# Attention scores of a hybrid decoder layer: two full-array matmuls in place of row-tiled passes

## The chip, the core and the metric

The kernel runs on one core of a Trainium2 chip. Five engines work side by side: TensorE (PE, the matrix engine, whose weight loads are listed apart as PEld), VectorE (DVE), ScalarE (ACT), GpSimd (POOL) and SyncE (SP), which here issues the DMAs. The metric is device time in microseconds of the whole program; lower is better. The times given are medians of separate runs, and a profile is one execution, so the two differ slightly.

## What is computed

One decoder layer on 1024 tokens of width 1024 in float32. One input projection feeds two token mixers, differential attention and a Mamba-2 state-space scan (SSD); their outputs are gated, merged and projected back. The change touches the scores of the attention:

```python
q = rms_norm(q, q_norm_w)            # 8 heads x 2 maps, 64 features each
k = rms_norm(k, k_norm_w)
scores = jnp.einsum('bqhmd,bkhmd->bhmqk', qb, k) * ATTN_HEAD_DIM ** -0.5
scores = jnp.where(causal, scores, -jnp.inf)
p = jax.nn.softmax(scores, axis=-1)
a = p[:, :, 0] - lam * p[:, :, 1]
o = jnp.einsum('bhqk,bkhe->bqhe', a, v)
```

Each head has two maps (m = 0 and 1), each with its own 64 query and 64 key features, so a score has a contraction of only 64, while TensorE's array has 128 rows.

## The kernel before

**Exact parts.** Matmuls are to be as good as float32. A float32 value is split into a high part that the engine's one-pass format (`F32R`) holds exactly and a low part that is the difference, and a product is made of three matmuls: high by high, high by low, low by high (`mm3`, `steps3`). ScalarE makes the high part by a copy, VectorE the low part by a subtraction.

**Order.** All instructions are issued in an order that a planner, class `Plan`, works out while the program is built. Its clock `pl.t` is TensorE's: every `mm` (line 162) and `tp` (a transpose, line 171) adds its cost. `bulk` (line 1197) supplies the large projections; chains of small steps (attention, SSD, splitting of weights) are generators that yield the time at which their next step falls due, and a step that is due goes ahead of the bulk work. Buffers are rationed on the same clock by class `Slots`: `bigs` counts the 19 large SBUF tiles of 4 KB per partition (`NBIG`, line 33), `mids` the medium ones, `trs`, `scs` and `mms` the PSUM tiles for transposes, scores and projections, two of each. The engines themselves then run their queues in this order and wait only for their operands.

**Stages.** The projections of the eight attention heads come first, `att_proj(h)` (line 470): for each of eight token tiles, 24 matmuls of 512 columns into a PSUM tile `pma`, which holds q, k, v and the gate of the head. While head h is projected, the attention of the heads before runs between its matmuls. Then come the four SSD groups: `ssd_proj_z` (PSUM tile `pmz`, four large tiles `zs`), `ssd_proj_xbc` (PSUM tiles `pc`, six large tiles `cv`), and beside the next group's projections `ssd_core`, eight chunks, each with a large decay tile `ab` and a product in PSUM tile `pD`. Last come the gates (`pg`), the merged projections (`pf`) and the output projection (`po`); line 1156 makes the last tile of `po` in two halves.

**Attention of a head.** `att_evac` (line 497) copies a projected tile out and normalises q and k. `qk_stack` (line 518) runs for each half of the tokens (512): it transposes q and k to feature-major in a PSUM tile `pq`, whose partitions 0 to 63 belong to map 0 and 64 to 127 to map 1, and fills the operands of the scores. `att_proj` reserves seven large tiles for a head: `v`, `zg` (the gate), `qs` and `kh` for both maps, and `kl`. They are given back when the last block of the head is done.

- `qs[m]` stacks the high and the low part of q of map m over the 128 partitions (high on the map's own 64, low on the other 64).
- `kh[m]` has the high part of k of map m twice, once on each half of the partitions.
- `kl` has the low part of k, map 0 on partitions 0 to 63, map 1 on 64 to 127.

`att_core` (line 553) then spawns `att_block` for each of the four query blocks of 128 tokens in the half. A block (line 562) takes keys up to its own end, n = 128 to 1024 columns, in column blocks of up to 512 (lines 584 to 590): per map one matmul of `qs` and `kh` over all 128 rows, which gives high by high and low by high at once, and then per map one matmul of 64 rows, high part of q by `kl`. The two 64-row matmuls use different halves of the array's rows. After that VectorE masks the scores and finds the row maximum (line 572), ScalarE takes the exponential, the two maps are combined, transposed (`pa`), multiplied with `v` (`av`), normalised, gated and transposed (`pya`).

Of the kernel before, what the change touches and what calls it, by code (L numbers as in the profile page):

```python
# [8 lines left out]
F32 = mybir.dt.float32  # L9
F32R = mybir.dt.float32r  # L10
BF16 = mybir.dt.bfloat16
AF = mybir.ActivationFunctionType
ALU = mybir.AluOpType
AX = mybir.AxisListType

P = 128
S = 1024
# [12 lines left out]
C_ZS = 7168  # L30
C_DT = 9216
C_GATE = 9248
NBIG, NW, NRAW, NMID, NSM = 19, 9, 4, 12, 8
PACE = 13.0
WPOOL = 3
XAHEAD = 3
HOP = 0.12
# [1 line left out]


class Slots:
    """Reuse times of a ring of buffers on the planned clock."""

    def __init__(self, n):
        self.free = [0.0] * n
# [11 lines left out]


class Plan:
    """One order for all engines: steps of dependent chains as their inputs fall due on a planned  # L60
    clock (the tensor engine's), bulk matrix work between them."""

    def __init__(self):
        self.t = 0.0
# [42 lines left out]
def tile_hybrid_layer(ctx: ExitStack, tc: tile.TileContext, x, norm_w, w_in, q_norm_w, k_norm_w,  # L107
                      diff_lambda, subln_w, conv_w, conv_b, dt_bias, a_log, d_skip, ssd_norm_w,
                      w_proj_attn, w_proj_ssd, w_out, out):
    nc = tc.nc  # L110
# [3 lines left out]
    const = ctx.enter_context(tc.tile_pool(name="const", bufs=1))  # L114
# [16 lines left out]

    pl = Plan()
    bigs, mids, sms = Slots(NBIG), Slots(NMID), Slots(NSM)
    trs, scs, mms = Slots(2), Slots(2), Slots(2)
    ws, raws = Slots(NW), Slots(NRAW)

    def bigt(shape, dt=F32, name="b"):
        return big.tile(shape, dt, tag="b4", name=name)
# [19 lines left out]
    def hpt(name):  # L158
        return hpool.tile([P, KB, S], F32R, tag="h", name=name)

# [1 line left out]
    def mm(o, lhsT, rhs, start, stop, after=0.0):  # L162
        nc.tensor.matmul(o, lhsT=lhsT, rhs=rhs, start=start, stop=stop)  # L163
        n, m = rhs.free_size(), lhsT.free_size()
        if rhs.dtype == F32:
            c = max(4 * n / 2400, 0.215)
        else:
            c = max(n / 2400 + 0.003, 0.057 if m <= 64 else 0.107)
        pl.t = max(pl.t, after) + c
# [13 lines left out]
    def in_ps(*aps):  # L183
        return any(a.space == bass.MemoryType.PSUM for a in aps)

    def act(o, i, f, after, **kw):
        nc.scalar.activation(o, i, f, **kw)  # L187
        c = 0.83e-3 * i.free_size() + (0.052 if in_ps(i) else 0.093) + 0.093 * (("accum_out" in kw) + any(not isinstance(kw.get(i, 0.0), float) for i in ("scale", "bias")))
        return pl.op("A", c, after)

    def tt(o, a, b, op, after, eng="V"):
        (nc.vector if eng == "V" else nc.gpsimd).tensor_tensor(out=o, in0=a, in1=b, op=op)  # L192
        n = o.free_size()
        return pl.op(eng, 0.07 + 1.042e-3 * n if eng == "V" else 0.095 + (1.77e-3 if op == ALU.mult else 2.22e-3) * n, after)

    def stt(o, a, s, b, op0, op1, after):
        nc.vector.scalar_tensor_tensor(out=o, in0=a, scalar=s, in1=b, op0=op0, op1=op1)  # L197
        return pl.op("V", 0.07 + 1.042e-3 * o.free_size() + (0.0 if isinstance(s, float) else 0.06), after)
# [21 lines left out]
        nc.gpsimd.tensor_tensor(out=dst, in0=dst, in1=mhalf[:, 0:cols], op=ALU.pow)  # L220
        return pl.op("G", 0.55 + 0.18 * cols, after)

# [1 line left out]
    mhalf = const.tile([P, 4], F32, name="mhalf")  # L224
    nc.gpsimd.memset(mhalf, -0.5)
    ident = const.tile([P, P], F32, name="ident")
# [12 lines left out]
    snc = lambda b: cols2[:, b:b + 1]  # L239
    sub_c, wqk_c, nlam_c = cols2[:, 16:17], cols2[:, 19:20], cols2[:, 20:21]  # L240
    hH, hL = hpt("hH"), hpt("hL")
    ready = {}

    def consts():
# [38 lines left out]
        trs.give(k, t1)  # L283
        ready["consts"] = stt(cols2[:, 19:20], cols2[:, 17:18], 8.0, cols2[:, 18:19], ALU.mult, ALU.mult, t1)

# [1 line left out]
    def att_w(h):  # L287
        return [(w_in[kb * P:(kb + 1) * P, 0:4096].rearrange("p (f c) -> p f c", f=4)[:, :, h * P:(h + 1) * P], 4, P)
                for kb in range(KB)]
# [84 lines left out]
        mm(o, a[1], b[0], False, last)  # L374
        yield

# [1 line left out]
    xts = {}  # L378
    h_at = {}

# [82 lines left out]
            if last and kb % 4 == 3:  # L463
                w_done(ids[kb // 4])

# [1 line left out]
    hd = {}  # L467
    lefts = {}

    def att_proj(h):  # L470
        ids = w_next(KB)
        ks = []
        for _ in range(7):
            ks.append((yield from pl.get(bigs)))
        v = bigt([P, NT, P], name=f"v{h}")
        zg = bigt([P, NT, P], name=f"zg{h}")
        qs = [bigt([P, S], F32R, name=f"qs{h}{m}") for m in range(2)]
        kh = [bigt([P, S], F32R, name=f"kh{h}{m}") for m in range(2)]
        kl = bigt([P, S], F32R, name=f"kl{h}")
        hd[h] = (v, zg, qs, kh, kl, ks)  # L480
        lefts[h] = [NT, {}]
        qk = []
        for t in range(NT):
            k = yield from pl.get(mms)
            pm = mmt(f"pma{h}{t}")
            yield from proj_tok(pm, t, ids, t == NT - 1)
            if t % 2 == 0:
                km = yield from pl.get(mids)
                qk.append([midt([P, 2, 256], name=f"qk{h}{t}"), km, 0])
            pl.spawn(att_evac(h, t, pm, k, qk[-1][0][:, t % 2, :], qk[-1]), pe_done())  # L490
            if t % 4 == 3:
                pl.spawn(qk_stack(h, t // 4, qk), pl.t + 3.0)
                qk = []
            if h == 0 and t == 0:
                pl.spawn(consts())
# [20 lines left out]
        cell.append(t2)  # L516

    def qk_stack(h, half, qk):
        v, zg, qs, kh, kl, _ = hd[h]
        lo, hi = slice(0, 64), slice(64, P)  # L520
        cs = slice(half * 512, half * 512 + 512)
        while len(qk[0]) < 5 or len(qk[1]) < 5 or "consts" not in ready:
            yield pl.t + 0.2
        yield max(qk[0][3:] + qk[1][3:] + [ready["consts"]])
        done = []
        for isk in range(2):
            k = yield from pl.get(trs)
            pt = trt(f"pq{h}{half}{isk}")
            for i in range(4):
                tp(pt[:, i * P:(i + 1) * P], qk[i // 2][0][:, i % 2, isk * P:(isk + 1) * P])  # L530
            if isk:
                for c in qk:
                    mids.give(c[1], pl.t + 0.1)
            at = pe_done()
            yield at
            t1 = at
            for m, (own, other) in enumerate(((lo, hi), (hi, lo))):
                if isk:
                    act(kh[m][own, cs], pt[own], AF.Copy, at)
                    t1 = act(kh[m][other, cs], pt[own], AF.Copy, at)  # L540
                else:
                    t1 = act(qs[m][own, cs], pt[own], AF.Copy, at, scale=wqk_c[own])
            yield t1
            for m, (own, other) in enumerate(((lo, hi), (hi, lo))):
                if isk:
                    t1 = tt(kl[own, cs], pt[own], kh[m][own, cs], ALU.subtract, t1 - HOP)
                else:
                    t1 = stt(qs[m][other, cs], pt[own], wqk_c[own], qs[m][own, cs], ALU.mult, ALU.subtract, t1 - HOP)
            done.append(t1)
            trs.give(k, t1)  # L550
        pl.spawn(att_core(h, half), max(done))

    def att_core(h, half):
        for qb in range(half * 4, half * 4 + 4):
            while max(bigs.avail(2), scs.avail(2)) > pl.t:
                a = max(bigs.avail(2), scs.avail(2))
                yield a if a < INF else pl.t + 0.2
            pk = [bigs.take(), bigs.take()]
            pl.spawn(att_block(h, qb, pk))
            yield pl.t + 0.6  # L560

    def att_block(h, qb, pk):
        v, zg, qs, kh, kl, ks = hd[h]
        n = (qb + 1) * P
        qsl = slice(qb * P, n)
        pr, sums, ex = [], [], []

        def soft(m, sc, k, at):
# [14 lines left out]
        sc = [sct(f"sc{h}{qb}{m}") for m in range(2)]  # L583
        for j in range(0, n, 512):
            e = min(n, j + 512)
            for m in range(2):
                mm(sc[m][:, j:e], qs[m][:, qsl], kh[m][:, j:e], True, False)
            for m in range(2):
                own = slice(m * 64, m * 64 + 64)
                mm(sc[m][:, j:e], qs[m][own, qsl], kl[own, j:e], False, True)  # L590
        for m in range(2):
            pl.spawn(soft(m, sc[m], k[m], pe_done()), pe_done() + 0.01 * m)
        while len(ex) < 2:
# [1 line left out]
        at = max(ex)  # L595
# [8 lines left out]
        at = stt(pr[0][:, 0:n], pr[1][:, 0:n], cc, pr[0][:, 0:n], ALU.mult, ALU.add, at)  # L604
# [3 lines left out]
        for j in range(0, qb + 1, 4):  # L608
# [3 lines left out]
            pt = trt(f"pa{h}{qb}{j}")  # L612
# [21 lines left out]
        at = pe_done()  # L634
# [5 lines left out]
        at = act(av[:, P:2 * P], av[:, 0:P], AF.Square, at, accum_out=ss)  # L640
        trs.give(k, at)
        yield at
        f = tin(1, "f")
        at = rsqrt(f, ss, e1, at)
        yield at
        at = stt(y, y, f, zg[:, qb, :], ALU.mult, ALU.mult, at)
# [16 lines left out]
        at = pe_done()  # L663
        yield at
        sms.give(kx, at)
        at = act(yt[0][:, (qb % 4) * P:(qb % 4 + 1) * P], py[:, 0:P], AF.Copy, at)
        trs.give(k, at)
        yt[2] += 1
        if yt[2] == 4:
            yield at  # L670
            at = load(ya_d[h * P:(h + 1) * P, qb // 4 * 512:qb // 4 * 512 + 512], yt[0], at)
# [10 lines left out]
        return  # L682
        yield

# [1 line left out]
    dtt = const.tile([P, NT, SH], F32, name="dtt")  # L686
    nac = const.tile([P, NT, SH], F32, name="nac")
    eac = const.tile([P, NT, SH], F32, name="eac")
# [99 lines left out]
        for i in km:  # L788
            mids.give(i, at)

# [1 line left out]
    gx, gz, ssd_n = {}, {}, {}  # L792

    def ssd_proj_xbc(g):
# [237 lines left out]
        if last:  # L1032
            ready["ssd", g] = at

# [1 line left out]
    def gates():  # L1036
        for ob in range(16):
            ids = w_next(2)
# [16 lines left out]
            bigs.give(cell[1], at)  # L1055
            ready["gate", ob] = at

# [1 line left out]
    yh = {}  # L1059

    def load_ys(half, lo, hi):
# [206 lines left out]
```

## Time and profile before

| | before |
|---|---|
| median of 3 runs | 1704.57 us (1703.73 to 1705.45) |
| span of the profiled execution | 1702.7 us |
| clock granted to TensorE in that execution | 1.000 of full speed |
| first and last score matmul starts, from the span's start | 57.7 and 610.7 us |
| score matmuls: 128 rows / 64 rows | 192 / 192 |

A row of the profile's timeline has the start, the time until the end of the last instruction in the row, the engine, line and operation, the tile written and the tiles read, the rows by columns of the array and the shape of the moving operand, the number of instructions, and in brackets the idle time just ahead with what ended it ("issue": nothing that the profile shows). Line 163 is `mm`, line 172 `tp`, line 187 `act`, whoever calls them, so rows are told apart by their tiles. In a table of windows each engine has its busy time and, as (x...), its instructions, in the order PE, PEld, DVE, ACT, POOL. A row of waits reads: who waited, for whom, us in total, times, longest.

### The profile page before, as it was taken

How to read it: one execution, taken by the hardware profiler on the slowest of the kernel's cores; microseconds unless marked ns; L12 is line 12 of the kernel's file. 1: busy time of each engine (PE TensorE's matmuls, PEld its weight loads, DVE VectorE, ACT ScalarE, POOL GpSimd, SP SyncE). 2: the span in 40 equal slices, each digit the busy share in tenths (PEclk: the TensorE clock that was granted, in tenths of full speed). 3: DMA queues.
4: the chain of work that ended last, by engine and by line, in shares of the span. 5: the costliest groups of instructions: out<-in, count | busy, mean ns of one | idle time of the engine just before them, and what ended most of it. 6: DMA issues, size and time to landing. Idle time of an engine off the chain costs nothing.

```text
span 1702.7 us, 23411 instructions
## 1 busy us (share of the span) xinstructions
PE 1682.2 (99%) x8370; PEld 1374.8 (81%) x8370; DVE 998.5 (59%) x1793; ACT 806.3 (47%) x1947; POOL 426.1 (25%) x541
## 2 busy tenths in 40 slices
PE   7999999999999999999999999999999999999999
PEld 5778778777787788888888888888888888887887
DVE  6676676666766645589578658847641243534332
ACT  5546556565564633365365455545542322424221
POOL 3323233232332201132243233323310011111110
PEclk9999999999999999999999999999999999999999
DMA  6202021120210203322142133224353444655442
GB/s 188 56 13 66 7 56 32 32 63 7 56 36 27 63 7 87 85 88 64 40 135 87 38 99 106 56 87 140 112 181 111 154 139 124 248 165 176 137 153 87
DMA packets 181986, 153.56 MB, mean 90 GB/s; under 512 B 9957, under 2 KB 149998, under 8 KB 181870
## 3 DMA queue, kind: packets, MB, share of 16 engines
q1 hardware_dynamic: 181870, 152.07, 29.3%
q8 instruction: 66, 1.08, 0.3%
q14 instruction: 50, 0.41, 0.1%
HBM read 126.74 MB, written 25.30 MB: 89 GB/s over the span
## 4 chain that ended last, share of the span: by engine, by line
PE 88%; DMA 3%; DVE 3%; issue 2%; POOL 2%; ACT 2%; SPq 1%; POOLq 0%; ACTq 0%; DVEq 0%
PE pma L163 19%; PE pc L163 15%; PE pf L163 12%; PE pg L163 9%; PE pmz L163 9%; PE sc L163 4%; PE av L163 4%; PE po L163 3%; PE pD L163 3%; PE pa L172 2%; DMA ry<-ys_d 1%; PE pS L163 1%; PE pO L163 1%; PE py L172 1%; PE pq L172 1%
## 5 line engine op out<-in xcount | busy, mean ns | idle before, releaser
L163 PE MATMUL pma<-w,hH 128*128 128x512 f32 x1024 | 342.5, 406 | 0.3 <-ACT hH L187 0.3
L187 ACT ACTIVATE w<-raw 128x512 fp32r<-128x512 f32 x306 | 191.0, 628 | 303.7 <-PE pf L163 146.2
L192 DVE TENSOR_TENSOR w<-raw,w 128x512 fp32r<-128x512 f32 (+1 forms) x207 | 156.4, 761 | 203.9 <-ACT w L187 201.8
L192 POOL TENSOR_TENSOR w<-raw,w 128x512 fp32r<-128x512 f32 (+1 forms) x99 | 134.8, 1362 | 552.8 <-ACT w L187 530.3
L163 PE MATMUL pc<-hH,w 128*128 128x512 f32 x768 | 243.7, 394 | 0.0
L163 PEld LDWEIGHTS pma<-w,hH 128*128 128x128 f32 x1024 | 189.4, 190 | 36.6 <-ACT hH L187 0.7
L163 PE MATMUL pma<-w,hL 128*128 128x512 f32 x512 | 209.9, 410 | 0.0
L163 PE MATMUL pf<-y,w 128*128 128x512 f32 x768 | 176.7, 389 | 0.0
L163 PEld LDWEIGHTS pf<-y,w 128*128 128x128 f32 x768 | 144.1, 188 | 30.0
L163 PEld LDWEIGHTS pc<-hH,w 128*128 128x128 f32 x768 | 142.9, 188 | 28.3
L163 PE MATMUL pmz<-w,hH 128*128 128x512 f32 x512 | 165.6, 397 | 0.0
L163 PE MATMUL pg<-hH,w 128*128 128x512 f32 x512 | 161.4, 393 | 0.0
L163 PE MATMUL pc<-hL,w 128*128 128x512 f32 x384 | 151.6, 395 | 0.0
L187 ACT ACTIVATE p<-p,nm 128x256 f32<-128x256 f32 (+7 forms) x128 | 98.1, 768 | 51.9 <-DVE nm L572 50.8
L163 PEld LDWEIGHTS pma<-w,hL 128*128 128x128 f32 x512 | 97.0, 189 | 18.7 <-issue 0.7
L163 PEld LDWEIGHTS pg<-hH,w 128*128 128x128 f32 x512 | 95.2, 188 | 18.8
L163 PEld LDWEIGHTS pmz<-w,hH 128*128 128x128 f32 x512 | 94.9, 188 | 18.6
L572 DVE CUSTOM_DVE_ANT_0 p<-sc,maskb 128x256 f32<-128x256 f32 (+7 forms) x128 | 91.7, 754 | 23.7 <-PE sc L163 23.2
L163 PE MATMUL pmz<-w,hL 128*128 128x512 f32 x256 | 101.1, 395 | 0.0
L163 PE MATMUL pg<-hL,w 128*128 128x512 f32 x256 | 100.5, 393 | 0.0
L197 DVE SCALAR_TENSOR_TENSOR cv<-pc,cols,cv 128x1023 f32<-128x1023 f32 (+2 forms) x72 | 91.8, 1275 | 12.1 <-ACT cv L187 11.5
L163 PE MATMUL pf<-yy,w 128*128 128x512 f32 x384 | 90.7, 390 | 0.9 <-DVE yy L197 0.9
(173 smaller groups left out, 2831.3 us busy)
## 6 DMA issues: line engine op xcount, KB each, us to landing
raw<-in_w_in_dram SPq DMA_DIRECT2D x176, 256.0 KB, 3.3
ab<-act_d SPq DMA_DIRECT2D x32, 512.0 KB, 4.3
raw<-in_w_proj_ssd_dram SPq DMA_DIRECT2D x64, 256.0 KB, 3.6
ys_d<-xdt SPq DMA_DIRECT2D x32, 256.0 KB, 3.2
gt_d<-gt SPq DMA_DIRECT2D x16, 512.0 KB, 5.0
ry<-ys_d SPq DMA_DIRECT2D x32, 256.0 KB, 6.3
raw<-in_w_proj_attn_dram SPq DMA_DIRECT2D x32, 256.0 KB, 3.4
gl<-gt_d SPq DMA_DIRECT2D x32, 256.0 KB, 3.8
```

What stands on the lines that cost most here:

```text
L163: nc.tensor.matmul(o, lhsT=lhsT, rhs=rhs, start=start, stop=stop)
L172: nc.tensor.transpose(out=o, in_=i, identity=ident if idn is None else idn)
L187: nc.scalar.activation(o, i, f, **kw)
L192: (nc.vector if eng == "V" else nc.gpsimd).tensor_tensor(out=o, in0=a, in1=b, op=op)
L197: nc.vector.scalar_tensor_tensor(out=o, in0=a, scalar=s, in1=b, op0=op0, op1=op1)
L572: nc.vector.tensor_tensor_reduce(out=p[:, 0:n], in0=sc[:, 0:n], in1=maskb[:, S - n:S], scale=-1.0, scalar=3e38, op0=ALU.add, op1=ALU.min, ...
```

## The change

The scores of a map and column block become two matmuls over all 128 partitions. For each map one large tile `kk[m]` has the high part of k on the map's own 64 partitions and the low part on the other 64. For each half of the tokens a large tile `qh` has the high part of q twice, on both halves of the partitions, and one of two fixed tiles `qlo` has the low part of q on the map's own partitions and zeros on the others. `qh` by `kk` gives high by high and high by low; `qlo` by `kk` gives low by high. The zeros are written once at the start. `att_proj` reserves four large tiles for a head instead of seven; `qk_stack` takes one more for `qh`, and a `qlo`, and both are given back after the scores of the half's last block. `NBIG` goes from 19 to 17. The diff also drops comments and docstrings (not shown).

```diff
-NBIG, NW, NRAW, NMID, NSM = 19, 9, 4, 12, 8
+NBIG, NW, NRAW, NMID, NSM = 17, 9, 4, 12, 8
...
-    trs, scs, mms = Slots(2), Slots(2), Slots(2)
+    trs, scs, mms, qlos = Slots(2), Slots(2), Slots(2), Slots(2)
...
+    qlo = [const.tile([P, 2, 512], F32R, name=f"qlo{i}") for i in range(2)]
+    for i in range(2):
+        nc.gpsimd.memset(qlo[i][64:P, 0].bitcast(F32), 0.0)
+        nc.gpsimd.memset(qlo[i][0:64, 1].bitcast(F32), 0.0)
...
     def att_proj(h):
...
-        for _ in range(7):
+        for _ in range(4):
             ks.append((yield from pl.get(bigs)))
...
-        qs = [bigt([P, S], F32R, name=f"qs{h}{m}") for m in range(2)]
-        kh = [bigt([P, S], F32R, name=f"kh{h}{m}") for m in range(2)]
-        kl = bigt([P, S], F32R, name=f"kl{h}")
-        hd[h] = (v, zg, qs, kh, kl, ks)
+        kk = [bigt([P, S], F32R, name=f"kk{h}{m}") for m in range(2)]
+        hd[h] = (v, zg, kk, ks)
...
     def qk_stack(h, half, qk):
...
+        kq = yield from pl.get(bigs)
+        kz = yield from pl.get(qlos)
+        qh, ql = bigt([P, 2, 512], F32R, name=f"qh{h}{half}"), qlo[kz]
...
                 if isk:
-                    act(kh[m][own, cs], pt[own], AF.Copy, at)
-                    t1 = act(kh[m][other, cs], pt[own], AF.Copy, at)
+                    t1 = act(kk[m][own, cs], pt[own], AF.Copy, at)
                 else:
-                    t1 = act(qs[m][own, cs], pt[own], AF.Copy, at, scale=wqk_c[own])
+                    act(qh[own, m], pt[own], AF.Copy, at, scale=wqk_c[own])
+                    t1 = act(qh[other, m], pt[own], AF.Copy, at, scale=wqk_c[own])
...
                 if isk:
-                    t1 = tt(kl[own, cs], pt[own], kh[m][own, cs], ALU.subtract, t1 - HOP)
+                    t1 = tt(kk[m][other, cs], pt[own], kk[m][own, cs], ALU.subtract, t1 - HOP)
                 else:
-                    t1 = stt(qs[m][other, cs], pt[own], wqk_c[own], qs[m][own, cs], ALU.mult, ALU.subtract, t1 - HOP)
+                    t1 = stt(ql[own, m], pt[own], wqk_c[own], qh[own, m], ALU.mult, ALU.subtract, t1 - HOP)
...
-        pl.spawn(att_core(h, half), max(done))
+        pl.spawn(att_core(h, half, (qh, ql, kq, kz)), max(done))
...
-        qsl = slice(qb * P, n)
+        qsl = slice(qb % 4 * P, (qb % 4 + 1) * P)
...
             for m in range(2):
-                mm(sc[m][:, j:e], qs[m][:, qsl], kh[m][:, j:e], True, False)
-            for m in range(2):
-                own = slice(m * 64, m * 64 + 64)
-                mm(sc[m][:, j:e], qs[m][own, qsl], kl[own, j:e], False, True)
+                mm(sc[m][:, j:e], qh[:, m, qsl], kk[m][:, j:e], True, False)
+                mm(sc[m][:, j:e], ql[:, m, qsl], kk[m][:, j:e], False, True)
+        if qb % 4 == 3:
+            bigs.give(kq, pl.t + 0.1)
+            qlos.give(kz, pl.t + 0.1)
```

More of the change, by code (lines that the diff above doesn't have):

```diff
@@ L518, in qk_stack @@
     def qk_stack(h, half, qk):
-        v, zg, qs, kh, kl, _ = hd[h]
+        v, zg, kk, _ = hd[h]
         lo, hi = slice(0, 64), slice(64, P)
@@ L545, in qk_stack, with att_core @@
                 if isk:
-                    t1 = tt(kl[own, cs], pt[own], kh[m][own, cs], ALU.subtract, t1 - HOP)
+                    t1 = tt(kk[m][other, cs], pt[own], kk[m][own, cs], ALU.subtract, t1 - HOP)
                 else:
-                    t1 = stt(qs[m][other, cs], pt[own], wqk_c[own], qs[m][own, cs], ALU.mult, ALU.subtract, t1 - HOP)
+                    t1 = stt(ql[own, m], pt[own], wqk_c[own], qh[own, m], ALU.mult, ALU.subtract, t1 - HOP)
             done.append(t1)
             trs.give(k, t1)
-        pl.spawn(att_core(h, half), max(done))
-    def att_core(h, half):
+        pl.spawn(att_core(h, half, (qh, ql, kq, kz)), max(done))
+    def att_core(h, half, q):
         for qb in range(half * 4, half * 4 + 4):
@@ L558, in att_core, with att_block @@
             pk = [bigs.take(), bigs.take()]
-            pl.spawn(att_block(h, qb, pk))
+            pl.spawn(att_block(h, qb, pk, q))
             yield pl.t + 0.6
-    def att_block(h, qb, pk):
-        v, zg, qs, kh, kl, ks = hd[h]
+    def att_block(h, qb, pk, q):
+        v, zg, kk, ks = hd[h]
+        qh, ql, kq, kz = q
         n = (qb + 1) * P
-        qsl = slice(qb * P, n)
+        qsl = slice(qb % 4 * P, (qb % 4 + 1) * P)
         pr, sums, ex = [], [], []
```

## The prediction

> **What bounds the kernel now.** I read the page's busy times and slices first, then its chain.
>
> ```profile
> span 1702.7 us, 23411 instructions
> PE 1682.2 (99%) x8370; PEld 1374.8 (81%) x8370; DVE 998.5 (59%) x1793; ACT 806.3 (47%) x1947; POOL 426.1 (25%) x541
> ...
> PEclk9999999999999999999999999999999999999999
> ...
> PE 88%; DMA 3%; DVE 3%; issue 2%; POOL 2%; ACT 2%; SPq 1%; POOLq 0%; ACTq 0%; DVEq 0%
> ```
>
> TensorE never rests for long, runs at full clock in every slice, and holds 88% of the chain that ended last. But 99% busy hides something: a matmul's modelled end reaches past the start of the next. What counts is the **pitch**, the distance between starts. So I went to the stage that the change touches and read the timeline, loads of weights included. Here is head 7, query block 7 (two column blocks of 512):
>
> ```profile
> 608.17 0.62 PE L163 MATMUL pmz<-w,hH 128*128 128x512 f32 x2
> ...
> 608.63 0.39 PE L163 MATMUL pmz<-w,hL 128*128 128x512 f32 x1
> ...
> 608.86 0.39 PE L163 MATMUL pmz<-w,hH 128*128 128x512 f32 x1
> 608.87 0.41 PEld L163 LDWEIGHTS sc<-kh,qs 128*128 128x128 f32 x2
> 609.09 0.61 PE L163 MATMUL sc<-kh,qs 128*128 128x512 f32 x2
> ...
> 609.63 0.18 PEld L163 LDWEIGHTS sc<-kl,qs 64*128 64x128 f32 x2 [0.35 <-issue]
> 609.63 0.50 PE L163 MATMUL sc<-kl,qs 64*128 64x512 f32 x2
> ...
> 610.06 0.30 PEld L163 LDWEIGHTS sc<-kh,qs 128*128 128x128 f32 x2 [0.25 <-issue]
> 610.07 0.74 PE L163 MATMUL sc<-kh,qs 128*128 128x512 f32 x2
> ...
> 610.73 0.49 PE L163 MATMUL sc<-kl,qs 64*128 64x512 f32 x2
> 611.15 0.33 PE L172 MATMUL pya<-ident,y 128*128 128x128 f32 x1
> ```
>
> Four full-array matmuls of 512 columns go from 608.17 to 609.09: 0.92 us, 0.23 each, because the weights of the next are loaded while the last one streams (608.87, ahead of 609.09). The row-tiled pair is different. Its two matmuls do run together (one row, 0.50 us for both), but their weights start only at 609.63, with the matmuls themselves, after 0.35 us in which the loader waited for nothing shown; and the full-array weights behind them again start with their matmul, at 610.06. So a column block costs two passes, a gap, one shared pass and another gap. From 610.07 to 611.15 that is 1.08 us for four matmuls, more than four full passes.
>
> ```profile
> PEld sc L163 <- issue: 29.0, 96, 0.4
> ```
>
> The list of waits says that this is the rule: 96 such gaps of the weight loader, 0.30 us each, and `sc` is filled in 96 column blocks, one gap each.
>
> **The change part by part.** First the scores. How many blocks of each width:
>
> ```profile
> L163 PE MATMUL sc<-kh,qs x192: 220/388/501, 57.7 to 610.4; 128*128 128x512 f32 x96, 128*128 128x128 f32 x32, 128*128 128x256 f32 x32, 128*128 128x384 f32 x32
> ```
>
> Two such matmuls stand in a block, so there are 48 blocks of 512 columns and 16 each of 384, 256 and 128. The new form issues the same number of matmuls (four), all over 128 partitions, so nothing is added to the count; what changes is that the pair becomes two full passes and both gaps should go.
>
> 512 columns: the second block above took 1.08 us (with the first block's trailing gap, without its own). The first took 0.98 from 609.09 to 610.07, and its trailing gap shows as the next pair of `kh` passes, 0.66 us in place of 0.54: 1.10 together. Against 0.92 that is 0.16 and 0.18; I take 0.17, times 48 = **8.2 us**.
>
> For the narrow blocks, and for what narrow full-array matmuls cost:
>
> ```profile
> 57.67 0.33 PE L163 MATMUL sc<-kh,qs 128*128 128x128 f32 x2
> 57.93 0.33 PE L163 MATMUL sc<-kl,qs 64*128 64x128 f32 x2
> 58.19 0.74 PE L163 MATMUL pma<-w,hH 128*128 128x512 f32 x2
> 58.77 0.40 PE L163 MATMUL pma<-w,hL 128*128 128x512 f32 x1
> ...
> 59.24 0.39 PE L163 MATMUL sc<-kh,qs 128*128 128x256 f32 x2
> 59.56 0.38 PE L163 MATMUL sc<-kl,qs 64*128 64x256 f32 x2
> 59.87 0.50 PE L163 MATMUL pma<-w,hH 128*128 128x512 f32 x1
> 60.21 0.40 PE L163 MATMUL pma<-w,hL 128*128 128x512 f32 x1
> ```
>
> ```profile
> 61.14 0.51 PE L163 MATMUL sc<-kh,qs 128*128 128x384 f32 x2
> 61.58 0.44 PE L163 MATMUL sc<-kl,qs 64*128 64x384 f32 x2
> 61.95 0.33 PE L172 MATMUL pa<-ident,p 128*128 128x128 f32 x1
> 62.04 0.71 PE L163 MATMUL pma<-w,hH 128*128 128x512 f32 x2
> 62.59 0.40 PE L163 MATMUL pma<-w,hL 128*128 128x512 f32 x1
> ...
> 68.40 0.61 PE L163 MATMUL av<-v,at 128*128 128x128 f32 x4
> 68.76 0.48 PE L163 MATMUL pma<-w,hH 128*128 128x512 f32 x1
> 69.08 0.27 PE L172 MATMUL pya<-ident,y 128*128 128x128 f32 x1
> ...
> 1687.67 11.80 PE L163 MATMUL po<-w,mg 128*128 128x512 f32 x74
> ```
>
> 128 columns, full array: the four `av` matmuls and the pass behind them take 68.40 to 69.08, 0.68 us; less 0.23 for that pass, 0.45 for four. Now: 57.67 to 58.19 is 0.52, and the next two passes take 0.58 where two take 0.46: 0.64. Saved 0.19, times 16 = **3.0**. 256 columns: of the 74 matmuls in the last row, line 1156 makes the final 48 (two halves of 24) 256 wide. The row ends with the end of its last matmul, 0.28 us long, so 11.52 us of starts less 26 x 0.23 leaves about 0.115 each, 0.47 for four with an edge. Now: 0.63 us, then 0.34 for a pass of 0.23: 0.74. Saved 0.27, times 16 = **4.3**. 384 columns: no other full-array row has this width; halfway between 0.115 and 0.23 gives 0.175 (an estimate), 0.70 for four. Now: 61.14 to 62.59 is 1.45, less a transpose (0.11) and two passes (0.46): 0.88. Saved 0.18, times 16 = **2.9**.
>
> Sum: 8.2 + 3.0 + 4.3 + 2.9 = **18.4 us**. All of it is TensorE's own pitch in a stage where it has no slack, so it comes off the end one for one, if the other engines follow. Bounds of this term: if only the gap ahead of the pair goes (609.09 to 609.63 is 0.54 where two passes take 0.46), 0.08 x 96 = 7.7 us; if the loader's whole idle time goes, 29.0 us. I stay with the sum, which is read off blocks of all four widths.
>
> Do the others follow? A stretch of attention, and two rows that matter for the moved work:
>
> ```profile
> 410.00:480.00 70.00, 70.00 (x374) 55.61 (x373) 46.44 (x118) 40.85 (x120) 21.70 (x35) 1.00 0.13 38
> ...
> L187 ACT ACTIVATE qs<-pq,cols x32: 670/684/686, 51.5 to 586.9; 64x512 fp32r<-64x512 f32 x32
> ...
> PE pya L172 <- DVE y L197: 2.3, 3, 0.9
> ```
>
> In 70 us VectorE (third column) works 46.44 and ScalarE 40.85; 2 to 3 us less room per stretch leaves both below 70%. `qk_stack` keeps six ScalarE copies and four VectorE differences per half: two plain copies of `kh` go and two scaled copies of q come. Even if nothing went, two at 0.684 us, 16 times, are 22 us on ScalarE over a stage of 550 us, beside TensorE's projections. The longer q chain delays its own first scores by about 1.4 us; `att_core` is spawned behind the whole stack, and projection matmuls of the next tiles stand in TensorE's queue meanwhile. I cost it at nothing; if that cover were gone it is 16 x 1.4 = 22 us. What is late next is the tail: `pya`, held by VectorE 2.3 us in all.
>
> The zeroing of `qlo` adds four GpSimd fills of 64 x 512 ahead of its first real work:
>
> ```profile
> 0.96 0.96 POOL L229 MEMSET maskb<- 128x1024 bf16 x1
> ...
> 5.41 0.55 POOL L407 TENSOR_TENSOR rs<-ss,mhalf 128x1 f32<-128x1 f32 x1 [2.91 <-DVE ss L197]
> ```
>
> By the row of `maskb` one fill is at most 0.96 us, likelier half: 2 to 3.8 us, into 2.91 us of idle. At worst the first normalisation is 0.9 us late. I take nothing. No DMA is added or moved, on SP's queue or any other.
>
> Buffers: a head holds four large buffers and one per half for q, where it held seven for its whole life, so attention is freer even with 17. One wait is new: VectorE's write of a `qlo` waits for the scores that read it two halves earlier, and VectorE's splits of weights would queue behind it. From the first to the last score, 57.7 to 610.4 in the `sc` row above, lie 16 halves, so two are some 70 us apart: the wait is long over. The SSD stage still wants what it wanted. By the code a group's projections of z meet six convolution tiles and the last two z tiles of the previous group, its two decay tiles (`ab`), and six convolution tiles and two z tiles of its own. Where I place token tile 2 of group 1, that is 18 of 17:
>
> ```profile
> 806.67 0.62 PE L163 MATMUL pmz<-w,hH 128*128 128x512 f32 x2
> 807.12 1.89 PE L163 MATMUL pD<-xdt,ab 128*128 128x64 f32 x16
> ```
>
> One tile is short until the chunk whose `pD` starts at 807.12 gives its decay tile back, behind 1.89 us. So a planned wait of up to 3 us, once or in each of three groups: 0 to 9 us. It is a wait of the planner's clock, and TensorE needs no such buffer before the result is evacuated, so I take the near end, 0.
>
> Forecast: 1702.7 - 18.4 = 1684.3 us of span. The median of the runs, 1704.57, is 1.9 us above the span; so **1686.2 us**.
>
> **The rivals.** (a) *The gaps stay* and only the sharing goes: **slower**. If the 0.35 us of loader idle came not from the switch to half-array tiles but from something that the new form keeps (the change of weights, accumulating into the same bank), a block pays its gaps and one pass more: 48 x 0.23 + 16 x (0.175 + 0.115 + 0.11) = 17.4 us, 1722. It decides once more than 0.17 us of gap, the saving, stays in a block of 512. For it: the pair really does share one pass. Against it: `pma`, `pmz` and `po` change weights at every pass and accumulate into one bank at a pitch of 0.23. Chance 0.05.
>
> The Trainium skill speaks for this side: "TensorE: Matmul & The Clock Gate", Part 3: Packing small matmuls, The mechanism, has matmuls in different row groups run at once and their weights pulled ahead, so that leaving the tiles would cost a pass. The trace agrees on the first half (two matmuls in 0.50 us) and not on the second (weights 0.35 us late). In the same skill "TensorEngine Tiling (Array Packing)", Key Properties, says that changing the tiling mode drains TensorE, which would put both gaps down to the tiles; a saving on the forecast's side, where the other page's rule ends at 1722.
>
> (b) *The gain is partly given back* by the ring of 17 in the SSD stage (up to 9 us) or by softmax chains that no longer keep pace: 1690.5 to 1697. For: 18 wanted of 17. Against: VectorE and ScalarE under 70%. Chance 0.13.
>
> (c) *More comes off*: with fewer buffers held, heads overlap more, and waits such as that of `pya` and the loader's 29.0 us go altogether: 1704.6 - 29 = 1675.6, range to 1681. Chance 0.09.
>
> (d) *Nothing to be seen*: (b) with nearly the whole gain lost. Chance 0.03.
>
> **How the numbers follow.** Forecast 1686.2, with 1681 to 1690.5 as its own range: 0.70. The range for 8 in 10 leaves out (a), (d) and the far ends of (b) and (c): 1677 to 1696. Changes below 0.2% (3.4 us) can't be told from none. Faster 0.91: forecast, (c) and most of (b). Same 0.04. Slower 0.05.
>
> **What would show it.** `sc` rows all 128*128, none with an "issue" wait of 0.3 at its loader; a block of 512 at 0.92 us from start to start; attention's stretch shorter by 17 to 20 us and every later stage as long as before. I am wrong if full-array `sc` matmuls keep a gap, if `sc` or `pya` gets waits on ScalarE or VectorE, or if the SSD stretch grows.

## The result and the profile after

The changed kernel takes 1721.07 us (median of 4 runs, 1720.36 to 1722.97) against 1704.76 us of the kernel before on the same chip: a ratio of 1.010, 95% interval 1.0085 to 1.0114. It is slower by 16.3 us, where 18.4 us less were forecast. The span of its profiled execution is 1718.6 us.

The page after, the same parts as were shown of before:

```profile
span 1718.6 us, 23446 instructions
PE 1680.0 (98%) x8370; PEld 1398.5 (81%) x8370; DVE 1003.9 (58%) x1793; ACT 809.0 (47%) x1947; POOL 428.5 (25%) x545
...
PEclk9999999999999999999998999899999999999999
...
PE 83%; DVE 5%; issue 3%; ACT 3%; DMA 3%; POOL 2%; SPq 0%; POOLq 0%; ACTq 0%; DVEq 0%
```

The instructions of TensorE are as many as before, yet its share of the chain fell from 88% to 83%, and the clock, which was full everywhere, dips in two slices, 902 to 945 and 1074 to 1117 us. Both lie in the SSD stage, whose code the change leaves as it was. So first the stage that it does touch, a block of 512 columns in the timeline:

```profile
62.79 0.19 PEld L163 LDWEIGHTS sc<-kk,qh 128*128 128x128 f32 x1
...
63.02 0.39 PE L163 MATMUL sc<-kk,qh 128*128 128x512 f32 x1
63.02 0.19 PEld L163 LDWEIGHTS sc<-kk,qlo 128*128 128x128 f32 x1
...
63.25 0.40 PE L163 MATMUL sc<-kk,qlo 128*128 128x512 f32 x1
...
63.48 0.39 PE L163 MATMUL sc<-kk,qh 128*128 128x512 f32 x1
...
63.72 0.40 PE L163 MATMUL sc<-kk,qlo 128*128 128x512 f32 x1
...
63.95 0.27 PE L172 MATMUL pa<-ident,p 128*128 128x128 f32 x1
```

Four passes from 63.02 to 63.95, 0.93 us, each with its weights loaded during the pass before. The gaps are gone. Adding the distances from start to start over all 384 score matmuls and the one matmul behind each block gives 99.2 us before and 80.9 us after: 18.3 us less, the sum that was forecast.

Where it is lost shows in the first and last starts of two projections, `pc` (first of the SSD stage with convolution) and `pg` (the gates, behind it). Before:

```profile
L163 PE MATMUL pc<-hH,w x768: 387/389/481, 641.1 to 1080.7; 128*128 128x512 f32 x192
...
L163 PE MATMUL pg<-hH,w x512: 387/389/481, 1137.5 to 1347.6; 128*128 128x512 f32 x171
```

After:

```profile
L163 PE MATMUL pc<-hH,w x768: 387/389/481, 628.9 to 1087.0; 128*128 128x512 f32 x192
...
L163 PE MATMUL pg<-hH,w x512: 387/389/481, 1153.7 to 1364.3; 128*128 128x512 f32 x171
```

Up to the first `pc` the changed kernel is 12.2 us ahead (so 6.1 of the 18.3 are already gone); from there to the first `pg` it takes 524.8 us in place of 496.4, 28.4 more; afterwards the two run alike. -18.3 + 6.1 + 28.4 = 16.2, against 15.9 between the spans.

The 28.4 us arise at three places (the stalls, from here on), each where the last `pc` matmul of a group is followed by its first `pmz`: 7.7, 14.5 and 13.2 us from one to the other, where the kernel before has 0.2. Together that is more than 28.4, because the matmuls of a chunk, due anyway, run in the stalls. The second place, on TensorE before:

```profile
937.70 0.39 PE L163 MATMUL pc<-hH,w 128*128 128x512 f32 x1
937.93 0.63 PE L163 MATMUL pmz<-w,hH 128*128 128x512 f32 x2
```

After:

```profile
932.71 0.39 PE L163 MATMUL pc<-hH,w 128*128 128x512 f32 x1
932.94 0.60 PE L172 MATMUL py<-ident,xn 128*128 128x128 f32 x4
933.37 0.63 PE L172 MATMUL px<-ident,cv 128*128 128x128 f32 x4
935.17 0.47 PE L163 MATMUL pO<-sh,ch 128*128 128x512 f32 x1 [1.17 <-ACT ch L187]
935.48 0.40 PE L163 MATMUL pO<-sl,ch 128*128 128x512 f32 x1
936.87 0.80 PE L163 MATMUL pO<-sh,cl 128*128 128x512 f32 x1 [0.99 <-DVE cl L192]
939.95 0.76 PE L163 MATMUL pS<-xh,bh 128*128 128x512 f32 x1 [2.28 <-DVE xl L192]
...
943.83 3.64 PE L163 MATMUL pD<-xdt,ab 128*128 128x64 f32 x16 [1.12 <-DVE bl L192]
947.24 1.20 PE L163 MATMUL pmz<-w,hH 128*128 128x512 f32 x2
```

No projection matmul stands in TensorE's queue between 932.71 and 947.24, only a chunk of the scan, whose steps wait for ScalarE and VectorE in turn. From 640 to 1140 us TensorE's listed waits add up to 15.3 us here and to 0.4 us in the kernel before. The waits name those engines, but what is missing is the bulk work that used to stand between the steps. That order was fixed when the program was built. The clock also drops: a stretch of this stage, before and after, with the clock after the five engines' busy times:

```profile
925.00:965.00 40.00, 40.00 (x220) 34.22 (x219) 35.01 (x48) 20.43 (x49) 12.82 (x15) 1.00 0.22 69
```

```profile
925.00:965.00 40.00, 34.27 (x172) 28.25 (x172) 30.78 (x43) 19.69 (x48) 11.72 (x14) 0.83 0.15 46
```

### The profile page after: what moved, and what is told of

It is laid out like the page before. It is cut to its first block, busy times and chain, and to the rows that moved or that the text cites. A ratio compares the mean times of both kernels' runs of the same rounds, so it can differ in the third digit from the quotient of the medians.

```text
span 1718.6 us, 23446 instructions
## 1 busy us (share of the span) xinstructions
PE 1680.0 (98%) x8370; PEld 1398.5 (81%) x8370; DVE 1003.9 (58%) x1793; ACT 809.0 (47%) x1947; POOL 428.5 (25%) x545
## 4 chain that ended last, share of the span: by engine, by line
PE 83%; DVE 5%; issue 3%; ACT 3%; DMA 3%; POOL 2%; SPq 0%; POOLq 0%; ACTq 0%; DVEq 0%
PE pma L163 16%; PE pc L163 14%; PE pf L163 14%; PE pmz L163 9%; PE pg L163 9%; PE sc L163 4%; PE po L163 4%; PE av L163 3%; PE pD L163 3%; PE pa L172 2%; DMA raw<-in_w_in_dram 1%; DVE w L192 1%; PE pS L163 1%; PE pq L172 1%; PE pO L163 1%
```

## The experiments

Two theories to start with. RING: with 17 places for large buffers in place of 19, the plan makes the z projection wait for a place. PHASE: attention ends earlier and otherwise, and the chunks fall badly. All times below are medians; the kernel before took 1702.9 to 1703.7 beside these runs.

**e1: 19 places again for the SSD stage.** The two `qlo` come from the ring and go back after the last score; attention still has 17.

```diff
-NBIG, NW, NRAW, NMID, NSM = 17, 9, 4, 12, 8
+NBIG, NW, NRAW, NMID, NSM = 19, 9, 4, 12, 8
-    qlo = [const.tile([P, 2, 512], F32R, name=f"qlo{i}") for i in range(2)]
+    klo = [bigs.take() for _ in range(2)]
+    qlo = [bigt([P, 2, 512], F32R, name=f"qlo{i}") for i in range(2)]
...
             qlos.give(kz, pl.t + 0.1)
+            if (h, qb) == (HEADS - 1, 7):
+                for i in klo:
+                    bigs.give(i, pl.t + 0.1)
```

> The changed kernel, with the two qlo tiles taken from the ring of large buffers (19 again) and given back to it after the last score, so that attention has 17 as before and the SSD stage has 19. Theory RING (the stalls of the SSD stage come from 17 large buffers in place of 19): the three stretches in which TensorE waits ahead of the z projections of groups 1 to 3 go, no half clock in the SSD stage, and about 1692.5 us, that is the time before less the 12.2 us by which the changed kernel is ahead when the first convolution projection starts (628.9 against 641.1). Rival PHASE (attention ends earlier and in another order, so the chunks fall otherwise against the projections, and the buffers are not the cause): the stalls stay, about 1721 us.

1691.26 us, ratio 0.993 (0.9914 to 0.9947). RING's number. The same place in e1's timeline, `pmz` right behind `pc`, and the stretch of windows at full clock:

```profile
925.72 0.39 PE L163 MATMUL pc<-hH,w 128*128 128x512 f32 x1
925.95 0.63 PE L163 MATMUL pmz<-w,hH 128*128 128x512 f32 x2
926.42 0.60 PE L172 MATMUL py<-ident,xn 128*128 128x128 f32 x4
926.77 0.48 PE L163 MATMUL pmz<-w,hL 128*128 128x512 f32 x1
```

```profile
925.00:965.00 40.00, 40.00 (x218) 34.12 (x217) 28.45 (x41) 16.33 (x38) 9.30 (x12) 1.00 0.14 40
```

**e2: the shortage alone, in the kernel before.** Two places are taken in the plan and never given back; the memory is there, only the order changes.

```diff
+        yield from pl.get(bigs, 2)
         yield from ssd_proj_z(0)
```

> The kernel before, scores row-tiled as they were, but from the first z projection on two of the 19 places of the large buffers are withheld in the plan (no memory is taken away, the order of the instructions alone changes). RING: the same three stalls appear, 25 to 35 us, about 1730 to 1740 us. PHASE: nothing moves in the SSD stage, 1704 to 1706 us.

1735.59 us (one run), 32.0 over its neighbour. The old scores, the old phase, and the same stalls (8.6, 14.5 and 13.2 us) and clock:

```profile
925.00:965.00 40.00, 34.06 (x163) 27.86 (x162) 33.67 (x45) 20.61 (x48) 12.90 (x14) 0.83 0.24 73
```

PHASE falls. And since no buffer was physically missing, the loss is the plan's order.

**e3: the four passes alone, in the kernel before.**

```diff
-                mm(sc[m][:, j:e], qs[m][own, qsl], kl[own, j:e], False, True)
+                mm(sc[m][:, j:e], qs[m][:, qsl], kh[m][:, j:e], False, True)
```

> The kernel before, buffers and qk_stack untouched, but the second matmul of each map takes all 128 partitions of qs and kh again in place of the 64-row pass with kl (so the product with the low part of k is left out and another is added twice). It has the changed kernel's four full passes and nothing else of it. Both theories of the scores expect 18.3 us less for the score matmuls themselves. If the 6 us that the changed kernel gives back inside attention come from chains that a faster TensorE overtakes: about 1692.5 us. If they come from the new operands and their buffers: about 1686.5 us.

1685.38 us, ratio 0.9896 (0.9877 to 0.9916): 18.2 us less than before. The faster scores give nothing back of themselves; the 6 us come from something else in attention.

**e5: is it the half clock?** While a z projection waits in the plan, TensorE gets matmuls that nobody needs.

```diff
-            if t % 2 == 0:
-                kb_ = yield from pl.get(bigs)
-                zs.append([bigt([P, 2, 512], name=f"zs{g}{t}"), kb_, 0])
             k = yield from pl.get(mms)
             pm = mmt(f"pmz{g}{t}")
+            if t % 2 == 0:
+                while bigs.avail(1) > pl.t:
+                    mm(pm, hH[:, 0, 0:P], hL[:, 0, 0:512], True, True)
+                    yield
+                kb_ = bigs.take()
+                zs.append([bigt([P, 2, 512], name=f"zs{g}{t}"), kb_, 0])
```

> The changed kernel, but while a z projection waits for a large buffer TensorE is given idle matmuls of 512 columns into the PSUM tile that the projection is about to overwrite, so that it stays busy and keeps its clock. If the half clock (30.8 us of it in the SSD stage of the changed kernel's trace) is a large part of the loss: 1706 to 1712 us, the clock 1.000. If the wait for the buffer alone sets the loss and the half clock falls on time that is idle anyway: 1718 to 1724 us.

1725.78 us, ratio 1.0134 (1.0113 to 1.0154): 5 us worse than the change, just above the higher of the two expectations. Its page counts the extra matmuls, and the stretch is now full and at full clock:

```profile
PE 1698.1 (98%) x8509; PEld 1415.3 (82%) x8509; DVE 1001.3 (58%) x1793; ACT 808.0 (47%) x1947; POOL 431.3 (25%) x545
```

```profile
925.00:965.00 40.00, 40.00 (x218) 34.10 (x218) 34.23 (x46) 19.98 (x46) 13.70 (x16) 1.00 0.24 73
```

139 more than 8370, at 0.23 us, are 32 us: the plan's waits measured in matmuls, and about the whole loss. So a full clock does not bring the time back when the waits are filled. The second and third stall last 14.4 and 13.6 us, about as long as in the changed kernel; the first, 20.4 us, goes on past one `pD` to the next. But the filling itself stands in TensorE's queue, so this run can't show what the half clock adds where nothing is filled in. Some it adds: in the changed kernel the first 20 passes behind the three stalls, which wait for nothing, take 8.8 us from start to start; at 0.23 us each they would take 4.6, so some 4 of the 28.4 us are slow passes behind the stalls (an estimate). How much it adds inside them stays open.

**e1b: 18 places.** e1 with `for i in klo[:1]`, so that one place comes back.

> e1, but only one of the two places comes back after attention, so the SSD stage is planned with 18 large buffers. RING, if each missing buffer costs its share: half of the 29 us, about 1706 us. RING, if the stage needs 18 or 19 only for moments (a wait of a few us): 1692 to 1697 us. If the count did not matter: 1691.3 us.

1691.29 us, ratio 0.9927 (0.9898 to 0.9956), as e1. The count is a step: 18 cost nothing, 17 cost 28 us.

**j1 and j2: who holds the 18th place?** j1 is the changed kernel, 17 places throughout, with at most two decay tiles in a group; j2 the same limit in e1.

```diff
         abs_ = {}
+        abl = Slots(2)
...
         def load_ab(c):
+            ka = yield from pl.get(abl)
             k = yield from pl.get(bigs)
...
-            abs_[c] = (ab, k, t)
+            abs_[c] = (ab, (k, ka, abl), t)
...
-        bigs.give(kab, pl.t + 0.1)
+        bigs.give(kab[0], pl.t + 0.1)
+        kab[2].give(kab[1], pl.t + 0.1)
```

> The changed kernel with 17 large buffers throughout, but an SSD group may hold two decay tiles at a time, not three: the next is loaded only after the one before the last has been used. If the 18th place is wanted for a third decay tile, loaded ahead while the z projection goes without: the three waits ahead of the z projections shrink, 1692 to 1700 us, less what later decay tiles cost. If the shortage is of another kind (the convolution and z tiles alone outgrow 17): 1718 to 1724 us.

> Control for j1: the same limit of two decay tiles in e1, where 19 places are free in the SSD stage. Its distance from e1 (1691.3 us) is the cost of loading decay tiles later. If the limit itself is harmless: 1690 to 1693 us; if chunks wait for their decay tile: up to 1710 us.

j1 takes 1692.58 us, ratio 0.994 (0.9917 to 0.9963); j2 1689.38, ratio 0.9917 (0.9888 to 0.9946). With 17 places and one load less ahead, all but 3 us of the loss is gone. In j1 `pmz` follows `pc` at once:

```profile
924.94 0.39 PE L163 MATMUL pc<-hH,w 128*128 128x512 f32 x1
925.17 0.62 PE L163 MATMUL pmz<-w,hH 128*128 128x512 f32 x2
```

So the place that z lacked was held by a third decay tile, loaded early for a chunk that did not yet need it. In the code `load_ab` is a step that is due, and due steps go ahead of `bulk`, so it takes a free place before z does. The second stall of the changed kernel shows the third tile: at the last `pD` ahead of the stall one more decay tile is loaded, and GpSimd masks it in the middle of the stall.

```profile
924.06 1.89 PE L163 MATMUL pD<-xdt,ab 128*128 128x64 f32 x16
...
924.44 0.50 SPq L209 DMA_DIRECT2D ab<-act_d  x1
...
937.74 1.10 POOL L863 TENSOR_SCALAR_AFFINE_SELECT ab<-ab 128x1024 f32<-128x1024 f32 x1
```

At that time the products `pD` of three chunks (943.83, 956.18 and 960.96) are still to come, each with its decay tile. The projection starts right behind the first of them, at 947.24; so too at the other two stalls, where `pD` starts at 785.09 and 1096.06 and `pmz` at 787.46 and 1100.21.

**g1 and g2: the 6 us in attention.** g1 is e3 with the changed kernel's instructions in `qk_stack`:

```diff
-                    act(kh[m][own, cs], pt[own], AF.Copy, at)
-                    t1 = act(kh[m][other, cs], pt[own], AF.Copy, at)
+                    t1 = act(kh[m][own, cs], pt[own], AF.Copy, at)
                 else:
-                    t1 = act(qs[m][own, cs], pt[own], AF.Copy, at, scale=wqk_c[own])
+                    act(qs[m][own, cs], pt[own], AF.Copy, at, scale=wqk_c[own])
+                    t1 = act(kl[other, cs], pt[own], AF.Copy, at, scale=wqk_c[own])
...
-                    t1 = tt(kl[own, cs], pt[own], kh[m][own, cs], ALU.subtract, t1 - HOP)
+                    t1 = tt(kh[m][other, cs], pt[own], kh[m][own, cs], ALU.subtract, t1 - HOP)
```

> The kernel before with four full passes as in e3, its buffers and reservations, but with the ScalarE and VectorE instructions of the changed kernel's qk_stack: four scaled copies for q (the second pair goes into kl, which nothing reads) and two plain ones for k, the low part of k written into kh. One product, low part of q by low part of k, is added and one is taken twice, so the scores differ from the reference's. If the 6 us that the changed kernel gives back inside attention come from these instructions (q holds its transpose buffer longer): about 1691 us. If they come from the buffers (fewer reserved, so blocks run otherwise): about 1685.5 us, as e3.

1691.73 us, ratio 0.9935 (0.9912 to 0.9958), 6.3 us over e3 (1690.32 to 1694.16 against 1685.29 to 1685.48): it is these instructions. The waits of TensorE and its loader from 40 to 640 us, first e3:

```profile
PE pya L172 <- DVE y L197: 3.3, 5, 1.0
...
PEld pq L172 <- ACT yt L187: 0.7, 2, 0.4
```

then g1:

```profile
PE pya L172 <- DVE y L197: 3.0, 5, 0.9
PE pq L172 <- DVE qk L192: 1.8, 3, 1.3
```

```profile
PEld pq L172 <- ACT yt L187: 3.4, 6, 0.6
PEld pq L172 <- DVE qk L192: 2.5, 3, 1.5
```

New or longer are the waits ahead of `pq`, the transposes of q and k. g2 holds e1 to two pairs of probability tiles:

```diff
+    prs = Slots(2)
...
-            while max(bigs.avail(2), scs.avail(2)) > pl.t:
+            while max(bigs.avail(2), scs.avail(2), prs.avail(1)) > pl.t:
...
-            pk = [bigs.take(), bigs.take()]
+            pk = [bigs.take(), bigs.take(), prs.take()]
...
         bigs.give(pk[0], pl.t + 0.1)
+        prs.give(pk[2], pl.t + 0.1)
```

> e1 with the attention blocks in flight held to two pairs of probability tiles, which is what 19 large buffers with two heads of seven leave. If the 6 us come from blocks that start earlier because more buffers are free: about 1685.5 us. If they come from the instructions of qk_stack: 1690 to 1693 us.

1695.05 us, ratio 0.9951 (0.9929 to 0.9974): 4 us above e1, outside both expectations. Free buffers in attention are no cause of the 6 us; they help.

**h2 and h3: which part of `qk_stack`?** The second copy of q's high part is made from SBUF, once the PSUM tile is given back, by ScalarE (h3) or by GpSimd (h2, `nc.gpsimd.tensor_copy`):

```diff
-                    act(qh[own, m], pt[own], AF.Copy, at, scale=wqk_c[own])
-                    t1 = act(qh[other, m], pt[own], AF.Copy, at, scale=wqk_c[own])
+                    t1 = act(qh[own, m], pt[own], AF.Copy, at, scale=wqk_c[own])
...
             trs.give(k, t1)
+            if not isk:
+                for m, (own, other) in enumerate(((lo, hi), (hi, lo))):
+                    t1 = max(t1, act(qh[other, m], qh[own, m], AF.Copy, t0))
```

(`t0` is the end of the first copies.)

> e1, but the second copy of the high part of q is made from qh in SBUF after the transposes' PSUM tile has been read and given back; ScalarE makes as many copies as in e1. If the 6 us come from the PSUM tile of the q transposes being held through four ScalarE copies: 1685 to 1687 us. If they come from ScalarE's own order and load, whichever memory it reads: 1690 to 1692 us.

> As h3, but GpSimd makes the second copy, so ScalarE is relieved of two copies per half as well. PSUM tile held: 1685 to 1687 us, as h3. ScalarE's load: better than h3 by up to 5 us. If GpSimd's share in the splits of weights or in the norms becomes late: above e1, over 1692 us.

h3 takes 1690.21 us (1687.81 to 1691.0), ratio 0.9921 (0.9904 to 0.9937), hardly less than e1; h2 1687.76 (1686.23 to 1688.79), ratio 0.9909 (0.9895 to 0.9924). Giving the PSUM tile back early is not it; taking the copies off ScalarE gains some 3 of the 6 us. In h3 the loader's wait for ScalarE at `pq` is back at 0.7 us, as in e3, but another wait for ScalarE, ahead of `pya`, has come; at h2 that one is 0.4 us. First h3, then h2:

```profile
PEld pya L172 <- ACT pma L187: 4.2, 4, 1.7
PEld pq L172 <- DVE qk L192: 2.3, 3, 1.2
```

```profile
PEld pq L172 <- DVE qk L192: 2.4, 3, 1.2
```

Where the other 3 us go is not shown. One wait that e3 does not have stays in all of g1, h3 and h2: `pq` waits 2.3 to 2.5 us for `qk`, which VectorE normalises. It may be the rest; no run tests it.

**k1: what helped, together** (e1, h2 and j2's limit).

> The parts that helped, together: four full passes, the two qlo tiles from the ring and back (e1), the second copy of q by GpSimd (h2), at most two decay tiles (j2). If what they save adds up, h2's 1687.8 us less the 1.9 us between e1 and j2: 1686 us. If they save the same time twice: 1688 us.

1687.31 us (1686.45 to 1688.35), ratio 0.9906 (0.989 to 0.9923). It does not add up beyond h2, from which it can't be told apart; both are the fastest versions here that compute the whole scores, 15 to 16 us under before and about 33 under the change.

## Why the prediction was wrong

- **Scores: right.** Forecast 18.4 us less, from four widths. The starts in the trace give 18.3, e3 alone 18.2. The gaps belonged to the half-array pair, as rows with them only around `kl` suggested. One reading beside the sum was off: the loader's 96 gaps are not one for each column block. 64 of them stand ahead of `kl`, in the blocks of 512 and 384 columns alone (21.2 us), and 32 ahead of `kh`, between the two column blocks of a query block (7.8 us). The sum did not use that count.
- **Buffers: the step that failed.** The prediction counted 18 wanted of 17, called it "a planned wait of up to 3 us, once or in each of three groups: 0 to 9 us", and took 0, because "TensorE needs no such buffer before the result is evacuated". It measured 28.4 us, and the sign that the prediction named last, a longer SSD stretch, is what came. Three things were wrong. The count had two decay tiles in a group; the plan loads a third ahead, so the shortage comes at the first z tile, and with two (j1) nearly all of the loss is gone. The price took the wait to be the rest of one `pD`, behind which a place comes back; but a place that comes back goes to the next decay tile first (j1), so the projection waits for the `pD` after it, through much of a chunk with no projection between its steps: 7.7, 14.5 and 13.2 us. And the reason for taking 0 looked at the engine's operands and not at the plan: when `bulk` waits, its matmuls are ordered behind the chunk's steps, and TensorE, which takes them in that order, pays for it even where the memory is free (e2, 32.0 us).
- **q's copies: costed at nothing, measured 6 us** (g1). The named cover, projections in TensorE's queue, held for the scores: in g1 TensorE waits 0.3 us in all at `sc`. It was the transposes ahead of them that became late, by ScalarE's copies for about half of the 6 us (h2); the rest stays open. The 22 us named for the case without cover were too many.
- **The rivals.** (b) had the right place and a planned wait as its cause, but an end of 1697. With 28.4 us in place of 9, and the 6 us of q's copies, 1686.2 comes to about 1720.7, near the 1721.07 measured. (a) had the time that came, 1722, for a reason that the trace excludes: the gaps did not stay. A matching number is no proof of a mechanism. The chance of 0.05 for slower was all (a)'s; that (b) had no part in it followed from its price.
- The Trainium skill, "TensorEngine Tiling (Array Packing)", Key Properties, has TensorE drained at each change of tiling mode. The trace agrees so far as no gap is left at `sc` where the mode no longer changes (four passes in 0.93 us); it does not show whether the gaps before were a drain or weights loaded late for another reason of the 64-row form.

## What to carry to other kernels

Where an order is planned, a smaller ring costs not the wait for the buffer but all the work that is ordered behind that wait; look for who takes a place first when one comes back, and price the wait by when the last taker before you is served. Count the places at the tightest moment of every stage that shares the ring, not only of the stage that is edited: one place was worth nothing or 28 us. Memory that an edit needs in one stage can be lent by the ring and returned, which here turned 16 us lost into 12 us gained.

## What the runs showed of the hardware

In the second stall of the changed kernel the clock fell to half for about 13.6 us (a mean of 0.83 over the 40 us of the window). The drop lies between the pass at 935.48 (0.40 us) and the one at 936.87 (0.80), and from 850 us up to there the trace lists only two waits of TensorE, 1.17 and 0.99 us long. At half clock the sixteen `pD` matmuls took 3.64 us, at full clock 1.89. Keeping the clock up with idle matmuls did not make the kernel faster (e5); the drop still has a price, of which some 4 us behind the three stalls can be read off the starts.
